# Accumulating DMAs for the row additions of a transformer layer, a fourth raw tile, and follow-ups beside two blocks

## The chip, the core and the metric

The kernel runs on one core of a Trainium2 chip. The engines of the core work side by side, each through its own instruction queue in order: PE multiplies matrices, DVE (vector), ACT (scalar) and POOL (GpSimd) work on rows, SP issues DMAs. An instruction that waits for a semaphore holds up everything behind it on its queue. The metric is the device time of one execution in microseconds, lower is better.

## The reference

One layer in float32 over 2048 tokens of width 1024: a token mixer (sliding-window attention and a gated recurrence side by side), a cross-attention into 256 memory tokens, and a SwiGLU feed-forward part of width 2816. Each part sits between two RMS norms and is added to the residual stream `h`:

```python
y = jnp.concatenate([ya, yh.astype(ya.dtype)], axis=-1) @ w_out[l]
h = h + rms_norm(y, g_mix_post[l])
u = rms_norm(h, g_x_pre[l])
m = rms_norm(mem, g_mem[l])
y = cross_attention(u, m, wq_x[l], wk_x[l], wv_x[l], wo_x[l])
h = h + rms_norm(y, g_x_post[l])
u = rms_norm(h, g_ffn_pre[l])
y = (jax.nn.silu(u @ w_gate[l]) * (u @ w_up[l])) @ w_down[l]
h = h + rms_norm(y, g_ffn_post[l])
```

The three residual additions, and the sum over three chunks of the last product, are what the change moves to other hardware.

## The kernel before

**Arithmetic.** Every float32 operand of a matmul is split into a high and a low half of a reduced format (`split2`: the high half on ACT or POOL at L833 and L835, the low half, a subtraction, always on DVE at L836), and a product is three matmuls (L913 to L915). Operands called T (weights or feed-forward inputs) are built ahead and stay for a job; operands called S are streamed.

**Jobs and blocks.** From about 780 us on the program runs a list of jobs (`jobs`, `phases`): the mixer's output product, the attention scores, the attention values, the hidden layer for each half of the tokens (100% PE-bound, 1400 to 2200 us), and three down jobs, one for each chunk of the hidden width (6, 8 and 8 tiles of 128). Each of the first three and of the down jobs has eight blocks of 256 tokens. A block is a 2 x 2 scheme of matrix blocks: kind "s" uses seven products (Strassen-like, `seven`) with steps 1, 5, 6, 3, 7, 2, 4; kind "p" uses the plain eight in four steps (`eight`) and stands at the ends of jobs. `out(i, j, a, b)` empties one quarter of the result (two parts `a` and `b`) into row tiles `y[0]`, `y[1]` of 128 x 1024; the last quarter comes in the last step.

**Order around a block.** At the head of a block `stream` asks for the raw input of the next block: two tiles of 128 x 4 x 256 (`sraw`, three buffers). After each product step `upto` makes the S operands that are needed two steps on, one step of the follow-up generator of the block before (`after`) is taken, and half an operand T of a later step is built (`half`, out of row tiles that SP loads). A follow-up is drained at the end of the block beside which it ran. All row tiles come out of one pool of ten. This is program order; the framework's scheduler arranges each engine's queue after its own simulation, so that neighbours on a queue can stand the other way round.

**What the follow-ups do.** `mixed_block`: after the squares of the quarters ACT has the sums; POOL multiplies each quarter with the gain (`scaled`, L1187); then DVE scales by the inverse root and adds the residual row tile `x`, loaded by SP (L1210); the row goes to `h1_d`; ACT squares it again; PE transposes it (L1098) into the former `x` tile, and it goes to `h1t_d`. `value_block` is the same with `h1_d` as the residual (L1283), `h2_d` as the store, and a scaled copy in the former `x` tile (L1290) that is transposed to `u_d`. `down_block(c, ...)`: job 0 stores its rows to `y2_d`; job 1 loads those rows and adds them on POOL (L1388), then stores; job 2 loads and adds them on POOL, squares on ACT (L1161), loads the residual from `h2_d`, multiplies by gain and root on DVE (L1408), adds on POOL (L1409) and stores to the output, both in halves of 512 columns (`ffn_out`). The very last block (`end`) takes the rows of `y2_d` as an addend of the eviction on DVE (L930, L1364), and ends with a short chain: squares on ACT, two small operations and a power on POOL (L90, L92, L97), DVE, store.

All DMAs before are issued by SP (`load`, `store`).

Of the kernel before, what the change touches and what calls it, by code (L numbers as in the profile page):

```python
# [11 lines left out]
F32 = mybir.dt.float32  # L12
# [6 lines left out]
P = 128  # L19
T = 2048  # L20
D = 1024
# [27 lines left out]
class Layer:  # L49
# [137 lines left out]
    def mix(self):  # L187
        tc, I = self.tc, self.I
        kw = dict(reuse_waits="tile")
        with contextlib.ExitStack() as left:  # L190
# [5 lines left out]
            with (  # L196
# [5 lines left out]
                self.banks(at, "ps1", **MOST)  # L202
                u = self.in_first()
# [32 lines left out]
            with (  # L236
# [5 lines left out]
                self.banks(at, "ps3", **MOST)  # L242
                for _ in phases:
                    pass
# [621 lines left out]
    def streamed(self, load, nk, kind, engine=None):  # L866
# [3 lines left out]
        for j in range(2):  # L870
            self._n += 1
            t = self.ts.tile([P, 4, 256], F32, tag="raw", name=f"sraw_{self._n}", bufs=3)[:, :nk, :]
            load(t, j)
            raw.append(t)
# [105 lines left out]
    def phases(self, jobs, first, prologue=None):  # L980
# [105 lines left out]
        for _ in after:  # L1086
            pass
# [91 lines left out]
    def scaled(self, d, a, b, to, g):  # L1179
# [7 lines left out]
        nc.gpsimd.tensor_tensor(d, d, g, ALU.mult)  # L1187

    def mixed_block(self, n):
        nc = self.nc  # L1190
        y, x, ss = {}, {}, []

        def out(i, j, a, b):
# [9 lines left out]
            sl = slice(j * 512, (j + 1) * 512)  # L1203
            self.scaled(y[i][:, sl], a, b, ss[0][:, 2 * i + j:2 * i + j + 1], self.g_mix_post[:, sl])

        def after():
            r = self.rstds(ss[0])
            s2 = self.small("q_s", 4)
            for i in range(2):
                nc.vector.scalar_tensor_tensor(y[i], y[i], r[:, i:i + 1], x[i], ALU.mult, ALU.add)  # L1210
                self.store(self.h1_d[(n + i) * P:(n + i + 1) * P, :], y[i])
                yield
            for i in range(2):
# [4 lines left out]
            for i in range(2):  # L1218
                self.store_transposed(self.h1t_d, n + i, self.transposed(y[i], x[i]))
# [40 lines left out]
    def value_block(self, n):  # L1260
        nc = self.nc
        y, x, ss = {}, {}, []

        def out(i, j, a, b):
# [8 lines left out]
            if (i, j) == (0, 0):  # L1273
                for r in range(2):
                    x[r] = self.rows_of(self.h1_d, n + r)
            sl = slice(j * 512, (j + 1) * 512)
            self.scaled(y[i][:, sl], a, b, ss[0][:, 2 * i + j:2 * i + j + 1], self.g_x_post[:, sl])

        def after():
            r = self.rstds(ss[0])  # L1280
            s2 = self.small("q_s", 4)
            for i in range(2):
                nc.vector.scalar_tensor_tensor(y[i], y[i], r[:, i:i + 1], x[i], ALU.mult, ALU.add)  # L1283
# [148 lines left out]
```

## Time and profile before

| | us |
|---|---|
| median of three runs | 2697.66 (2691.52 to 2702.04) |
| the profiled execution | 2689.73 |
| its span | 2688.0 |
| mean granted clock of PE | 0.989 |
| DMA queue of SP: 450 MB | 51.2% of 16 engines' span |

Times in the profile's rows are microseconds from the start of the span. A row of the timeline gives start, duration, engine, line, operation, output and inputs, the count of merged instructions, and in brackets how long the engine had been idle and what ended that. A group row gives busy us and mean ns of one instruction, then the idle time before it and its releasers. A row `A <- B: t, n, m` of the waits says that A waited for B for t us in all, n times, at most m. A window row gives start and end, its length, and the busy time of each engine with its number of instructions. An issue row of the DMAs gives KB each and median us from issue to landing. `Lnnn` is a line of the kernel; DMAs issued by the helpers carry the helpers' lines L75 (load) and L78 (store).

### The profile page before, as it was taken

The page shows a single profiled execution, that of the slowest core. Times are in us where ns is not written, and L with a number is a line of the kernel's source. Part 1 is how long each engine was busy: PE and PEld are TensorE (multiplying, and loading weights), DVE is VectorE, ACT ScalarE, POOL GpSimd, SP SyncE. Part 2 cuts the span into 40 slices and gives each one's busy share as a digit, 9 for nine tenths or more (in the row PEclk, how much of TensorE's full clock was granted, in tenths as well). Part 3 has the DMA queues.
Part 4 walks back from the last instruction along what each step waited for, and adds up shares of the span by engine and source line. Part 5 has one row for each costly group of instructions (what it writes and reads, how often), then busy time and mean ns, then how long its engine had stood idle before and what let it go on. Part 6 is the DMA issues. An engine that isn't in the chain of part 4 may idle for free. (4 is left out here: it accounts for less than half of the span.)

```text
span 2688.0 us, 34731 instructions
## 1 busy us (share of the span) xinstructions
PE 2590.8 (96%) x12362; PEld 2155.6 (80%) x12362; DVE 1804.5 (67%) x2653; ACT 1236.4 (46%) x2585; POOL 660.7 (25%) x733
## 2 busy tenths in 40 slices
PE   7989999999989999999999999999999999999987
PEld 5878888887977787887778888888888888888765
DVE  7675578877545668687785555575555565676987
ACT  4453366655424566555563333353333343533432
POOL 5340344322533552234420000000000000032455
PEclk9999999999999999999999999999999999999998
DMA  5434655445878585385772222362222253846654
GB/s 176 137 124 165 191 155 159 131 142 170 252 238 243 194 288 190 111 265 190 247 252 79 86 90 81 96 235 86 79 79 87 87 197 131 290 168 249 237 185 167
DMA packets 396429, 452.26 MB, mean 168 GB/s; under 512 B 19296, under 2 KB 310112, under 8 KB 396256
## 3 DMA queue, kind: packets, MB, share of 16 engines
q1 hardware_dynamic: 396256, 450.05, 51.2%
q8 instruction: 97, 1.59, 0.3%
q14 instruction: 76, 0.62, 0.1%
HBM read 315.77 MB, written 134.22 MB: 167 GB/s over the span
## 5 line engine op out<-in xcount | busy, mean ns | idle before, releaser
L913 PE MATMUL psm<-T,S 128*128 128x512 f32 x2726 | 1064.4, 394 | 27.0 <-ACT part L928 13.4
L915 PE MATMUL psm<-T,S 128*128 128x512 f32 x2726 | 1058.8, 392 | 16.7 <-DVE S L836 16.6
L914 PE MATMUL psm<-T,S 128*128 128x512 f32 x2726 | 1066.5, 391 | 0.8 <-DVE T L836 0.8
L913 PEld LDWEIGHTS psm<-T,S 128*128 128x128 f32 x2726 | 514.9, 189 | 142.3 <-ACT part L928 17.2
L915 PEld LDWEIGHTS psm<-T,S 128*128 128x128 f32 x2726 | 515.2, 189 | 130.7 <-DVE S L836 23.2
L914 PEld LDWEIGHTS psm<-T,S 128*128 128x128 f32 x2726 | 515.2, 189 | 106.7 <-DVE T L836 1.4
L836 DVE TENSOR_TENSOR S<-sraw,S 128x512 fp32r<-128x512 f32 (+1 forms) x327 | 277.5, 856 | 230.9 <-ACT S L833 214.6
L1388 POOL TENSOR_TENSOR row<-row,row 128x1024 f32<-128x1024 f32 x30 | 84.6, 2829 | 1140.6 <-DVE row L856 980.6
L833 ACT ACTIVATE S<-sum 128x512 fp32r<-128x512 f32 (+1 forms) x288 | 173.0, 617 | 344.2 <-PE psm L915 247.2
L836 DVE TENSOR_TENSOR S<-sum,S 128x512 fp32r<-128x512 f32 (+1 forms) x340 | 249.3, 741 | 48.9 <-ACT S L833 30.4
L928 ACT ACTIVATE part<-psm 128x512 f32<-128x512 f32 x252 | 149.7, 596 | 214.5 <-PE psm L915 197.2
L833 ACT ACTIVATE S<-sraw 128x512 fp32r<-128x512 f32 (+1 forms) x274 | 168.6, 615 | 131.0 <-PE psm L915 119.4
L836 DVE TENSOR_TENSOR T<-row,T 128x1024 fp32r<-128x1024 f32 (+1 forms) x134 | 166.5, 1251 | 55.7 <-ACT T L833 54.7
L833 ACT ACTIVATE T<-row 128x1024 fp32r<-128x1024 f32 (+1 forms) x134 | 136.7, 1030 | 117.4 <-DVE row L853 25.8
L151 PE MATMUL psg<-u,whi 128*128 128x512 f32 x352 | 142.1, 404 | 1.7 <-POOL whi L135 1.7
L153 PE MATMUL psg<-u,wlo 128*128 128x512 f32 x352 | 140.2, 398 | 0.9 <-DVE wlo L136 0.9
L152 PE MATMUL psg<-u,whi 128*128 128x512 f32 x352 | 140.0, 398 | 0.0
L1161 ACT ACTIVATE junk<-row 128x512 f32<-128x512 f32 x160 | 99.8, 625 | 74.5 <-POOL row L1388 27.3
L1187 POOL TENSOR_TENSOR row<-row,g 128x512 f32<-128x512 f32 x64 | 97.8, 1537 | 111.2 <-ACT junk L1161 103.2
L888 DVE TENSOR_TENSOR sum<-sraw,sraw 128x512 f32<-128x512 f32 (+1 forms) x85 | 61.3, 721 | 43.3 <-DMA sraw<-hid_d 9.0
L1311 DVE TENSOR_TENSOR row<-psm,part 128x512 f32<-128x512 f32 x60 | 39.9, 688 | 68.3 <-PE psm L915 68.3
L135 POOL TENSOR_SCALAR whi<-raw 128x1024 fp32r<-128x1024 f32 x46 | 52.4, 1139 | 126.8 <-PE psg L152 36.4
(328 smaller groups left out, 3688.8 us busy)
## 6 DMA issues: line engine op xcount, KB each, us to landing
row<-in_w_down_dram SPq DMA_DIRECT2D x53, 512.0 KB, 7.0
sraw<-in_w_gate_dram SPq DMA_DIRECT2D x44, 512.0 KB, 3.8
row<-u_d SPq DMA_DIRECT2D x44, 512.0 KB, 7.6
sraw<-in_w_up_dram SPq DMA_DIRECT2D x44, 512.0 KB, 3.7
hid_d<-row SPq DMA_DIRECT2D x44, 512.0 KB, 2.6
h_d<-row SPq DMA_DIRECT2D x32, 512.0 KB, 2.7
row<-h_d SPq DMA_DIRECT2D x32, 512.0 KB, 5.9
y_d<-row SPq DMA_DIRECT2D x32, 512.0 KB, 3.5
```

Of the source, the lines that this page charges most:

```text
L151: nc.tensor.matmul(ps, ah, bh, start=(i == 0), stop=False)
L152: nc.tensor.matmul(ps, ah, bl, start=False, stop=False)
L153: nc.tensor.matmul(ps, al, bh, start=False, stop=(i == n - 1))
L833: self.nc.scalar.activation(hi, raw, AF.Copy)
L836: self.nc.vector.tensor_tensor(lo, raw, f32(hi), ALU.subtract)
L913: nc.tensor.matmul(ps, s[:, 0, k, :], t[:, 0, k, :], start=st, stop=False, **kw)
L914: nc.tensor.matmul(ps, s[:, 0, k, :], t[:, 1, k, :], start=False, stop=False, **kw)
L915: nc.tensor.matmul(ps, s[:, 1, k, :], t[:, 0, k, :], start=False, stop=sp, **kw)
L928: nc.scalar.activation(t, ps, AF.Copy)
L1161: self.nc.scalar.activation(junk, a, AF.Square, scale=float(D) ** -0.5, accum_out=to)
L1187: nc.gpsimd.tensor_tensor(d, d, g, ALU.mult)
L1388: nc.gpsimd.tensor_tensor(y[i], y[i], y2[i], ALU.add)
```

## The change

- A new helper `add` issues, from POOL's queue, a DMA that reads rows from HBM and adds them to a row tile already in SBUF. It takes the place of the loads of residual rows and of `y2_d` rows, and of the POOL additions at L1388 and L1409. Before it stands the DVE pass that applies root and gain in one instruction, and after it the store, which waits for it.
- The POOL gain multiply in `scaled` (L1187) goes; the function is called `squared` and the gain is applied in the DVE pass.
- Raw tiles: four buffers in the second part of the program instead of three; row tiles: nine instead of ten (both are 4 KB in a partition).
- Follow-ups form a list: each step takes one step of every follow-up still alive, and a follow-up isn't drained at the end of a block. The generators get empty steps between the additions and the squares, and in `value_block` before the transposes.
- In the last down job the last two blocks (`late`) take the `y2_d` rows as addends of the eviction instead of an accumulating DMA; the residual of the last block is still loaded and added on DVE. The last chain on POOL has two operations instead of three.

```diff
@@ mix
                 self.banks(at, "ps3", **MOST)
+                self.raws = 4
@@ phases
-        after = iter(())
+        after = []
...
                     for _ in range(1 if kind == "s" else 2):
-                        next(after, None)
+                        for f in list(after):
+                            if next(f, after) is after:
+                                after.remove(f)
                         half(g, self.row_tile)
                     g += 1
-                for _ in after:
-                    pass
-                after = follow()
+                after.append(follow())
@@ row_tile
-        return self.st_pool.tile([P, D], F32, tag="row", name=f"row_{self._n}", bufs=10)
+        return self.st_pool.tile([P, D], F32, tag="row", name=f"row_{self._n}", bufs=9)
@@ squared
         self.mean_square(d, to)
-        nc.gpsimd.tensor_tensor(d, d, g, ALU.mult)
+
+    def add(self, d, src, n):
+
+        self.nc.gpsimd.dma_start(d, src[n * P:(n + 1) * P, :], accum_op=ALU.add)
@@ mixed_block
-            if (i, j) == (0, 0):
-                for r in range(2):
-                    x[r] = self.rows_of(self.I["x"], n + r)
...
             for i in range(2):
-                nc.vector.scalar_tensor_tensor(y[i], y[i], r[:, i:i + 1], x[i], ALU.mult, ALU.add)
+                nc.vector.scalar_tensor_tensor(y[i], y[i], r[:, i:i + 1], self.g_mix_post, ALU.mult, ALU.mult)
+                self.add(y[i], self.I["x"], n + i)
                 self.store(self.h1_d[(n + i) * P:(n + i + 1) * P, :], y[i])
                 yield
+            yield
             for i in range(2):
                 self.mean_squares(y[i], i, s2)
                 yield
...
-                self.store_transposed(self.h1t_d, n + i, self.transposed(y[i], x[i]))
+                self.store_transposed(self.h1t_d, n + i, self.transposed(y[i], self.row_tile()))
@@ value_block
-                nc.vector.scalar_tensor_tensor(y[i], y[i], r[:, i:i + 1], x[i], ALU.mult, ALU.add)
+                nc.vector.scalar_tensor_tensor(y[i], y[i], r[:, i:i + 1], self.g_x_post, ALU.mult, ALU.mult)
+                self.add(y[i], self.h1_d, n + i)
                 self.store(self.h2_d[(n + i) * P:(n + i + 1) * P, :], y[i])
-                self.mean_squares(y[i], i, s2)
-                yield
-            r = self.rstds(s2)
+                yield
             yield
             for i in range(2):
-                nc.vector.scalar_tensor_tensor(x[i], y[i], r[:, i:i + 1], self.g_ffn_pre, ALU.mult, ALU.mult)
-                yield
+                self.mean_squares(y[i], i, s2)
+                yield
+            r = self.rstds(s2)
+            u = [self.row_tile() for _ in range(2)]
             for i in range(2):
-                self.store_transposed(self.u_d, n + i, self.transposed(x[i], x[i]))
+                nc.vector.scalar_tensor_tensor(u[i], y[i], r[:, i:i + 1], self.g_ffn_pre, ALU.mult, ALU.mult)
+                yield
+            yield
+            for i in range(2):
+                self.store_transposed(self.u_d, n + i, self.transposed(u[i], u[i]))
                 yield
@@ down_block
+        late = last and n >= NT - 4
...
-            if end:
+            if late:
                 for i in range(2):
                     y[i] = self.rows_of(self.y2_d, n + i)
...
-            elif end:
+            elif late:
                 nc.vector.tensor_tensor(d, a, d, ALU.add)
...
-                    r = self.rstd([ss[0][:, 2 * i + q:2 * i + q + 1] for q in range(2)], 1, "p")
+                    v = self.small("p_v")
+                    nc.gpsimd.tensor_scalar(v, ss[0][:, 2 * i:2 * i + 1], ss[0][:, 2 * i + 1:2 * i + 2], EPS,
+                                            ALU.add, ALU.add)
+                    r = self.small("p_r")
+                    nc.gpsimd.tensor_tensor(r, v, self.mhalf[:, 0:1], ALU.pow)
...
-                if y2:
-                    nc.gpsimd.tensor_tensor(y[i], y[i], y2[i], ALU.add)
...
+            for i in range(0 if late else 2):
+                if c:
+                    self.add(y[i], self.y2_d, n + i)
+                if not last:
+                    self.store(self.y2_d[(n + i) * P:(n + i + 1) * P, :], y[i])
+                yield
+            if last:
+                if not late:
+                    yield
+                for i in range(2):
                     self.mean_squares(y[i], i, s2)
...
+                yield
                 r = self.rstds(s2)
                 for i in range(2):
-                    self.ffn_out(n + i, y[i], x[i], r[:, i:i + 1])
+                    nc.vector.scalar_tensor_tensor(y[i], y[i], r[:, i:i + 1], self.g_post, ALU.mult, ALU.mult)
+                    self.add(y[i], self.h2_d, n + i)
+                    self.store(self.out[(n + i) * P:(n + i + 1) * P, :], y[i])
                     yield
 
-        return stream, out, after, part if end else None
+        return stream, out, after, part if late else None
```

More of the change, by code (lines that the diff above doesn't have):

```diff
@@ L871, in streamed @@
             self._n += 1
-            t = self.ts.tile([P, 4, 256], F32, tag="raw", name=f"sraw_{self._n}", bufs=3)[:, :nk, :]
+            t = self.ts.tile([P, 4, 256], F32, tag="raw", name=f"sraw_{self._n}", bufs=self.raws)[:, :nk, :]
             load(t, j)
@@ L1078, in phases @@
                     for _ in range(1 if kind == "s" else 2):
-                        next(after, None)
+                        for f in list(after):
+                            if next(f, after) is after:
+                                after.remove(f)
                         half(g, self.row_tile)
                     g += 1
-                for _ in after:
-                    pass
-                after = follow()
+                after.append(follow())
                 at += 1
-        for _ in after:
-            pass
+        for f in after:
+            for _ in f:
+                pass
     def transposed(self, y, t):
@@ L1272, in out @@
                     self.load(self.g_ffn_pre, self.I["g_ffn_pre"][0:1, :].broadcast_to([P, D]))
[L1273 to L1277, printed above, removed]
+            self.squared(y[i][:, j * 512:(j + 1) * 512], a, b, ss[0][:, 2 * i + j:2 * i + j + 1])
         def after():
@@ L1353, in out @@
                 y[i] = self.row_tile()
-            if c and not end and (i, j) == (0, 0):
-                for r in range(2):
-                    y2[r] = self.rows_of(self.y2_d, n + r)
             if end and not x:
```

26 lines of the change are left out of this document (7 added, 19 removed).

## The prediction

> **What bounds it.** I read the page's 40 slices first, then windows of 20 us, then the rows inside the bad windows.
>
> ```profile
> span 2688.0 us, 34731 instructions
> PE   7989999999989999999999999999999999999987
> POOL 5340344322533552234420000000000000032455
> ```
>
> PE is full nearly everywhere, so only stretches where it waits can be won. POOL returns in the last slices, where PE dips. The windows there (length, then busy us and instructions of PE, PE's weight loads, DVE, ACT and POOL; granted clock, DMA share, GB/s):
>
> ```profile
> 2500.00:2520.00 20.00, 20.00 (x90) 16.57 (x89) 17.71 (x17) 10.27 (x15) 7.76 (x2) 1.00 0.80 290
> 2520.00:2540.00 20.00, 15.37 (x59) 11.28 (x58) 19.88 (x21) 9.60 (x20) 12.67 (x9) 0.91 0.37 130
> 2540.00:2560.00 20.00, 20.00 (x90) 16.55 (x89) 17.83 (x18) 9.17 (x19) 12.41 (x9) 1.00 0.41 147
> 2560.00:2580.00 20.00, 17.58 (x77) 13.96 (x75) 15.82 (x14) 8.24 (x18) 11.44 (x9) 1.00 0.55 198
> 2580.00:2600.00 20.00, 16.54 (x71) 12.97 (x71) 15.92 (x17) 8.09 (x18) 10.08 (x8) 1.00 0.50 184
> 2600.00:2620.00 20.00, 16.49 (x70) 12.66 (x69) 16.81 (x16) 7.73 (x17) 11.06 (x8) 1.00 0.52 188
> 2620.00:2640.00 20.00, 16.40 (x69) 12.60 (x68) 16.05 (x16) 6.04 (x13) 11.79 (x8) 0.97 0.63 233
> 2640.00:2660.00 20.00, 20.00 (x78) 16.24 (x77) 15.19 (x16) 6.87 (x16) 12.20 (x9) 0.86 0.52 189
> 2660.00:2680.00 20.00, 14.23 (x54) 11.15 (x52) 14.61 (x15) 5.29 (x16) 11.38 (x11) 0.83 0.27 104
> ```
>
> The first is a full window: 90 matmuls in 20 us, 0.222 us each. The eight after it, the last down job, hold 59+90+77+71+70+69+78+54 = 568, worth 126.2 us at that pace; they take 160. So this job loses 33.8 us. Part of it shows as a lowered clock behind a gap, not as idle time, so I count matmuls.
>
> One such gap, then the engine groups from 2120 us on (busy us, mean ns):
>
> ```profile
> 2588.97 5.56 POOL L1388 TENSOR_TENSOR row<-row,row 128x1024 f32<-128x1024 f32 x2 [7.29 <-DMA row<-y_d]
> 2589.43 6.24 DVE L836 TENSOR_TENSOR S<-sraw,S 128x512 fp32r<-128x512 f32 x3
> 2592.32 0.50 PE L915 MATMUL psm<-T,S 128*128 128x512 f32 x1 [2.63 <-DVE S L836]
> 2666.66 4.78 DVE L1408 SCALAR_TENSOR_TENSOR row<-row,q_r,g 128x512 f32<-128x512 f32 x4 [0.69 <-POOL q_r L1176]
> 2667.49 6.30 POOL L1409 TENSOR_TENSOR row<-row,row 128x512 f32<-128x512 f32 x4 [0.87 <-DVE row L1408]
> 2675.09 0.77 PE L913 MATMUL psm<-T,S 128*128 128x512 f32 x1 [5.77 <-DVE row L1362]
> ...
> L836 DVE TENSOR_TENSOR S<-sraw,S 128x512 fp32r<-128x512 f32 x66 | 79.2, 1218 | 28.3 <-ACT S L833 28.1
> L888 DVE TENSOR_TENSOR sum<-sraw 128x512 f32<-128x512 f32 x16 | 11.0, 685 | 0.2
> L1408 DVE SCALAR_TENSOR_TENSOR row<-row,q_r,g 128x512 f32<-128x512 f32 x28 | 33.6, 1261 | 6.0 <-POOL q_r L1176 6.0
> L1409 POOL TENSOR_TENSOR row<-row,row 128x512 f32<-128x512 f32 x28 | 47.2, 1716 | 6.7 <-DVE row L1408 6.7
> ```
>
> While POOL adds two rows, three DVE subtractions take 6.24 us; alone one takes about 0.685, so 2.06. DVE stands still beside a POOL add, the low half of S comes late, and PE waits 2.63 us. The 5.77 us gap has the same neighbour: four gain multiplies on DVE beside four additions on POOL (L1408, L1409), and behind them on DVE the eviction that PE waits for.
>
> SP adds to it. Its waits between 2540 and 2680 us, and two blocks' first loads:
>
> ```profile
> SPq L78 <- POOL row L1409: 61.9, 20, 13.4
> ...
> 2582.89 0.38 SPq L75 DMA_DIRECT2D sraw<-hid_d  x1
> 2606.32 0.38 SPq L75 DMA_DIRECT2D sraw<-hid_d  x1
> ```
>
> Output stores block the queue until L1409 is done and the next raw tile is asked for behind them. A block takes 23.43 us; its 84 matmuls (7 products of 4 x 3) need 18.7.
>
> **The change, part by part.** *POOL row additions out* (L1388, L1409; L1187 in the two earlier jobs). In the last job a block drops about 2 x 2.8 + 4 x 1.7 = 12.4 us of POOL work. What ended PE's waits there was a DVE result late beside POOL, so most of the 33.8 us is within reach. I leave 3 us of the first window (new weights are built there, DVE 19.88 of 20 busy), 1 us in each of five blocks and 2 us at the end: 33.8 - 10 = **24 us won**. Bounds: 33.8 if all goes, 0 if DVE is held as long by what replaces it. Next in line is PE itself: undisturbed, DVE has 14 operations of 0.69 and two of 1.28 us in a block, 12.2 of 18.7.
>
> In the value job a block is 21.82 us:
>
> ```profile
> 1237.66 0.37 SPq L75 DMA_DIRECT2D sraw<-pt_d  x1
> 1259.48 0.37 SPq L75 DMA_DIRECT2D sraw<-pt_d  x1
> ...
> 1379.29 1.03 PE L1098 MATMUL pss<-ident,row 128*128 128x128 f32 x8
> L1283 DVE SCALAR_TENSOR_TENSOR row<-row,q_r,row x16: 1272/1280/1637, 1209.2 to 1366.7; 128x1024 f32<-128x1024 f32 x16
> L1187 POOL TENSOR_TENSOR row<-row,g 128x512 f32<-128x512 f32 x64 | 97.8, 1537 | 111.2 <-ACT junk L1161 103.2
> ```
>
> 84 matmuls and 16 transposes need 18.7 + 2.1 = 20.8 us, so 1.0 us is lost in each of six steady blocks. The four gain multiplies go off POOL and ride free in the DVE pass that added the residual (1.28 us, as L1283 now). I take half: **3 us** (0 to 6). The mixed job runs at full pace after 880 us; its one stall follows here, and I take 0 for it (0 to 5.5), since ACT stood there behind a weight tile that SP asked for only at 870.10:
>
> ```profile
> PE psm L913 <- ACT part L928: 5.5, 1, 5.5
> 870.10 0.37 SPq L75 DMA_DIRECT2D row<-in_w_out_dram  x1
> ```
>
> *74 accumulating DMAs in* (16 mixed, 16 value, 16 in the second down job, 12 + 14 in the last), issued from POOL. They replace as many 512 KB loads on SP, so HBM traffic stays. The trace has no such DMA. From below it is a plain load, from above two of the slowest, as it must read both sums: h_d rows land in 5.9 us, u_d rows in 7.6.
>
> ```profile
> row<-u_d SPq DMA_DIRECT2D x44, 512.0 KB, 7.6
> row<-h_d SPq DMA_DIRECT2D x32, 512.0 KB, 5.9
> out_dram<-row SPq DMA_DIRECT2D x32, 256.0 KB, 2.0
> ```
>
> So 5.9 to 15.2 us; I take 9, a load and a half, because these loads already share the engines. On POOL the issue costs at most what a small operation does (L90 0.76 us, below); it waits there for the DVE pass, and behind it on POOL stand the splits of S (L835) that the mixed and value jobs give to POOL. L1187 waited there for ACT instead, so I put the difference at 0.
>
> *New waits.* Two queues now wait for a landing. On ACT the squares (L1161): behind them stand the high halves of S and the copies that free PSUM. The code leaves three product steps between add and square in mixed and value, two for the second row in the last job, and S is made two steps ahead. A step is 12 x 0.222 = 2.67 us, so PE feels a landing later than 5 x 2.67 = 13.3 us, or 4 x 2.67 = 10.7. At 9 us nothing shows; I charge **2 us** for uneven landings (0 to 57, the top worked out below). On SP the stores wait for the landing; behind them stand raw and weight loads. The fourth raw tile lets both loads of a block go out a block ahead, 18.7 us against a 9 us hold: 0, but without that cover the late loads cost what they cost now, some of the 4.7 us a block.
>
> *The rest.* Nine row tiles for ten: a block no longer holds two residual tiles, so no tile is missed; 0. Follow-ups beside two blocks: only value's is longer than a block; its transposes move three steps on, and the next job reads the early blocks first; 0. The late blocks' addend goes to DVE's eviction as the last block's did; 0 with POOL quiet. The final chain drops one POOL operation:
>
> ```profile
> 2681.81 0.76 POOL L90 TENSOR_SCALAR p_v<-q_s 128x1 f32<-128x1 f32 x1 [3.67 <-ACT junk L1161]
> 2682.65 0.22 POOL L92 TENSOR_SCALAR p_w<-p_v 128x1 f32<-128x1 f32 x1
> ```
>
> 0.3 us. **Sum:** 24 + 3 - 2 + 0.3 = 25 us, span 2688 to 2663. That execution took 2689.73 us; the median of the runs, 2697.66, lies 7.9 above it. Taking the same 25 off the median gives 2672.
>
> The Trainium skill says, in SBUF — State Buffer, Who interferes with whom, that a DVE instruction with two SBUF inputs contends with a GpSimd instruction that reads SBUF; the 6.24 us above agree. The same page, SBUF: two separate sides, speaks against the change: descriptors of a GpSimd DMA are written by GpSimd and starve while DVE runs a 2-port operation, for which it gives about 3.1 us instead of 0.62. By that every add could come some 2.5 us later, an estimate from that page; 9 + 2.5 = 11.5 would touch only the last job.
>
> **Rivals.** *More than forecast:* the value loss and the mixed stall go whole, and the last job runs nearly clean: 33.8 + 6 + 5.5 = 45, so 2652. For: late weight rows came from a crowded row pool. Against: those jobs keep ACT and DMA as busy.
>
> *Given back:* stores that wait for landings hold SP so long that raw tiles stay late, and each of five or six blocks keeps its 4.7 us; the early jobs lose a little too. Net about -3, 2695. For: SP's 61.9 us behind L1409. Against: the fourth tile.
>
> *Slower:* the add is as slow as its upper bound, 15.2 us. ACT then stalls 15.2 - 13.3 = 1.9 us in 16 blocks and 4.5 us in six: 57 us against the 27 won, so +30 and 2728. It decides from 13.8 us of landing, where 16 x (L - 13.3) + 6 x (L - 10.7) is 27. For: in the mixed job the engines are already 78% busy:
>
> ```profile
> 880.00:1020.00 140.00, 140.00 (x667) 116.20 (x667) 93.78 (x102) 82.60 (x184) 71.33 (x91) 1.00 0.78 261
> ```
>
> Against: the last job's share is near 0.5.
>
> *It doesn't do what it says:* issuing a DMA holds DVE as an add did. At 0.76 us for four issues instead of 12.4 us that can keep at most a quarter; if issues were as long as L1409's 1.7, half the gain: 2686.
>
> **Numbers.** Forecast 0.60, more 0.10, given back 0.12, slower 0.14, no relief 0.04. What a measurement can tell from no change is 0.5%, 13.5 us. Faster: nearly all of 0.60, 0.10 and part of the last: 0.70. Same: 0.15, slower: 0.15. The likeliest case alone spans 2660 to 2686; the range reaches to the clean case below (2649) and partly into the slow one above, 2706.
>
> **What would show it.** Right: L836 and the gain multiplies near 0.69 and 1.3 us throughout, 84-matmul blocks of 19 to 20 us in the last job, no PE wait on L836 there, adds landing under 11 us. Wrong: PE or ACT waiting on rows that an add writes, SP stores held over 10 us, DVE operations still double.

## The result, and the profile after

The changed kernel takes 2686.02 us (median of 9 runs, 2680.87 to 2690.87) against 2698.03 (9 runs): a ratio of 0.9955, 95% interval 0.9942 to 0.9969. Forecast were 25 us (2672), measured are 12. The page of the changed kernel (span; POOL in 40 slices; packets, MB and share of each DMA queue, q1 for SP and q0 for POOL):

```profile
span 2683.9 us, 34591 instructions
...
POOL 5240344321431332223320000000000000000022
...
q1 hardware_dynamic: 383584, 411.25, 47.4%
q0 software_dynamic: 10656, 38.80, 8.2%
```

POOL is quiet in the last job now. Its windows, in the columns of the prediction:

```profile
2520.00:2540.00 20.00, 18.27 (x81) 14.81 (x79) 13.22 (x14) 9.41 (x13) 1.19 (x2) 1.00 1.03 339
2540.00:2560.00 20.00, 16.35 (x63) 13.37 (x64) 14.78 (x20) 10.17 (x20) 2.82 (x6) 0.83 0.51 112
2560.00:2580.00 20.00, 20.00 (x90) 16.56 (x89) 12.41 (x18) 9.84 (x21) 5.71 (x9) 1.00 0.88 213
2580.00:2600.00 20.00, 20.00 (x90) 16.55 (x89) 12.54 (x18) 9.05 (x19) 4.96 (x8) 1.00 0.88 214
2600.00:2620.00 20.00, 20.00 (x90) 16.57 (x89) 12.73 (x19) 9.05 (x19) 5.10 (x8) 1.00 1.03 272
2620.00:2640.00 20.00, 20.00 (x90) 16.58 (x89) 10.67 (x15) 8.45 (x18) 4.75 (x7) 1.00 0.96 253
2640.00:2660.00 20.00, 20.00 (x90) 16.57 (x89) 14.39 (x22) 9.04 (x21) 3.80 (x6) 1.00 0.84 197
2660.00:2680.00 20.00, 14.05 (x61) 11.00 (x60) 12.94 (x19) 4.95 (x14) 5.67 (x9) 0.94 0.80 216
```

From 2560 to 2660 us every window holds the full 90 matmuls, where before had 69 to 78. The engine groups from 2120 us on say why: the subtraction that took 1218 ns in the mean with POOL's additions beside it (L836, now L838) takes 690, and a pass over twice the columns with gain and root takes 1280, where the half pass took 1261.

```profile
L838 DVE TENSOR_TENSOR S<-sraw,S 128x512 fp32r<-128x512 f32 x69 | 47.1, 690 | 55.9 <-ACT S L835 55.8
L1407 DVE SCALAR_TENSOR_TENSOR row<-row,q_r,g 128x1024 f32<-128x1024 f32 x14 | 17.8, 1280 | 4.4 <-POOL q_r L1179 4.1
L1193 POOL DMA_DIRECT2D row<-h_d x14 | 12.8, 917 | 12.7 <-DVE row L1407 12.1 <-DVE S L838 0.6
```

The last row is the issue of an add: 0.92 us of POOL. The landings of the adds (KB each, median us):

```profile
row<-h_d POOLq DMA_DIRECT2D x30, 512.0 KB, 7.7
row<-y_d POOLq DMA_DIRECT2D x28, 512.0 KB, 6.8
row<-in_x_dram POOLq DMA_DIRECT2D x16, 512.0 KB, 7.7
```

The slowest of them took 12.2 us. In the last job nearly all this is as forecast or better, so something ahead of it was lost. It shows at the two places where a job hands over to the next: mixed to score, and value to hidden. Windows over the two, for the kernel before (a second execution, see below) and then for the changed one:

```profile
968.00:1068.00 100.00, 97.80 (x460) 79.95 (x459) 78.53 (x105) 60.28 (x129) 37.26 (x51) 1.00 0.75 255
1323.00:1433.00 110.00, 105.82 (x481) 85.47 (x480) 87.89 (x94) 63.97 (x119) 27.17 (x30) 1.00 0.70 238
```

```profile
968.00:1068.00 100.00, 91.61 (x421) 74.74 (x420) 67.77 (x83) 58.43 (x120) 32.40 (x45) 0.95 0.91 273
1323.00:1433.00 110.00, 100.12 (x449) 81.04 (x448) 75.29 (x84) 61.67 (x118) 20.82 (x32) 0.95 0.83 257
```

39 and 32 matmuls fewer in the same time, 71 x 0.222 = some 15.8 us, with the clock down behind the gaps and the share of the DMA engines up from 0.75 to 0.91 and from 0.70 to 0.83. What stood behind the gaps in the changed kernel's timeline:

```profile
1044.25 0.80 PE L915 MATMUL psm<-T,S 128*128 128x512 f32 x1 [4.99 <-ACT T L835]
...
1380.80 1.94 PE L1101 MATMUL pss<-ident,row 128*128 128x128 f32 x8 [3.68 <-ACT T L835]
1396.83 1.23 DVE L852 TENSOR_TENSOR row<-row,row 128x1024 f32<-128x1024 f32 x1 [4.04 <-DMA row<-u_d]
1405.58 0.79 PE L915 MATMUL psm<-T,S 128*128 128x512 f32 x1 [3.55 <-ACT S L835]
```

At the first hand-over PE waits for an operand T of the next job. T is built out of row tiles that SP loads (for the score job of `qk_d`, for the hidden job of `u_d`), and these land late. At the second the view names T in front of a transpose and S in front of a matmul; T and the high half of S are made on ACT's queue, which stands there for rows of `u_d` (7.9 us in all from 1340 to 1430).

**Where the time went, by stretch.** Cutting every profile into windows of 4 us and adding up their matmuls gives the time at which each kernel had done the same number of them (a matmul on a border counts twice, in all alike). The table gives, for each stretch (times are those of the reference execution), what a kernel lost (+) or won (-) against a second profiled execution of the kernel before (span 2690.7); the column of the last job is what is left to the difference of the spans. The experiments follow below.

| | to 779 | mixed to 968 | hand-over to 1144 | value to 1323 | hand-over to 1509 | to 2502 | last job | ratio of the runs |
|---|---|---|---|---|---|---|---|---|
| before, first execution | -5.7 | +0.1 | -1.2 | -0.3 | +1.2 | -1.0 | +4.2 | |
| changed | +6.8 | -0.6 | +8.5 | -5.4 | +9.2 | -2.3 | -23.0 | 0.9955 |
| e1 down jobs only | +5.7 | +0.8 | +0.4 | +0.6 | +2.6 | -0.9 | -22.2 | 0.9936 |
| e2 front jobs only | +3.4 | -2.0 | +7.6 | -4.6 | +8.1 | -0.4 | -4.7 | 1.0011 |
| e3 ten rows, three raws | +6.5 | -0.1 | +7.4 | +5.3 | +3.5 | -0.7 | -23.1 | 0.9986 |
| e4 before, nine rows, four raws | +2.5 | +1.1 | +2.9 | +2.3 | +0.6 | +0.1 | -1.1 | 1.0010 |
| e5 late stores in front | -2.3 | -2.0 | +7.5 | -4.9 | +9.7 | -0.9 | -22.4 | 0.9956 |
| e6 plain loads in front | +2.5 | -1.1 | +1.3 | -4.9 | +0.5 | -0.7 | -20.5 | 0.9888 |
| e8 down jobs only, late stores | +0.2 | +2.7 | +1.3 | +0.8 | +1.3 | +0.9 | -26.3 | 0.9942 |
| e9 plain loads and copies | +1.4 | -2.0 | +2.9 | +6.5 | +8.8 | -0.8 | -21.9 | 0.9985 |
| e10 early adds | +6.8 | +2.1 | +3.8 | -4.7 | +6.9 | -0.7 | -26.0 | 0.9925 |
| e11 early adds in value only | +8.6 | +1.5 | +1.6 | -4.8 | +6.5 | -0.9 | -28.6 | 0.9934 |
| e12 order only | +4.7 | +2.9 | +4.1 | +4.4 | +2.7 | -3.7 | -22.3 | 0.9943 |
| e13 early adds, order of before | +6.7 | -1.4 | +1.8 | -5.7 | +6.9 | -0.7 | -22.1 | 0.9911 |
| e14 stores from ACT | +8.7 | -2.6 | +11.4 | +4.6 | +10.0 | -3.0 | -20.3 | 0.9995 |
| e15 e13, stores from ACT | +0.6 | -0.2 | +2.8 | +1.6 | +6.8 | -0.7 | -21.1 | 0.9945 |

In the first 779 us, where the edits hardly touch the program, executions lie 14 us apart, so I read from there on: the changed kernel wins 23.0 + 5.4 + 0.6 + 2.3 = 31.3 and loses 17.7 at the hand-overs, together 13.6. The medians say 12.0. Each row is one execution. How far a figure scatters is seen in the two executions of before (1.2 us at a hand-over, 4.2 in the last job) and in e5, whose stores turned out to stand where those of the changed kernel do (0.5 to 1.0 at the hand-overs). The cut at 779 us falls where PE waits, so the first two columns of a row can trade some 2 us.

The second hand-over has to be read together with the value job before it. The changed kernel wins 5.4 there and loses 9.2 behind it, 3.8 in all; e1, with no lead from the value job, loses 3.2 in all, and e6 wins 4.4. So against before, more than half of the 9.2 takes back what the value job had won; against plain loads in the same places the adds cost 3.8 + 4.4 = 8.2 us there, and 8.5 - 1.3 = 7.2 at the first hand-over.

### The profile page after: what moved, and what is told of

It is laid out like the page before. It is cut to its first block, busy times and chain, and to the rows that moved or that the text cites. A ratio compares the mean times of both kernels' runs of the same rounds, so it can differ in the third digit from the quotient of the medians.

```text
span 2683.9 us, 34591 instructions
## 1 busy us (share of the span) xinstructions
PE 2588.4 (96%) x12362; PEld 2162.3 (81%) x12362; DVE 1691.2 (63%) x2643; ACT 1236.3 (46%) x2581; POOL 500.3 (19%) x683
## 4 chain that ended last, share of the span: by engine, by line
PE 79%; DMA 9%; DVE 3%; POOL 3%; issue 3%; ACT 2%; SPq 1%; POOLq 0%; DVEq 0%; ACTq 0%
PE psm L917 21%; PE psm L915 21%; PE psm L916 21%; PE psg L153 2%; PE psg L151 2%; PE psg L152 2%; DMA row<-in_w_down_dram 1%; PE pss L1101 1%; DMA row<-h_d 1%; DMA row<-in_w_out_dram 1%; DMA row<-in_x_dram 1%; DMA z<-in_w_out_dram 1%; DMA row<-u_d 1%; DVE S L838 0%; DMA h1t_d<-row 0%
## 5 line engine op out<-in xcount | busy, mean ns | idle before, releaser
L838 DVE TENSOR_TENSOR S<-sraw,S 128x512 fp32r<-128x512 f32 (+1 forms) x327 | 228.8, 704 | 253.8 <-ACT S L835 234.4
L838 DVE TENSOR_TENSOR S<-sum,S 128x512 fp32r<-128x512 f32 (+1 forms) x340 | 229.6, 685 | 62.7 <-ACT S L835 38.9
L930 ACT ACTIVATE part<-psm 128x512 f32<-128x512 f32 x249 | 147.5, 597 | 224.5 <-PE psm L917 209.3
L1193 POOL DMA_DIRECT2D row<-y_d x28 | 25.9, 926 | 1136.8 <-DVE T L838 971.7
L838 DVE TENSOR_TENSOR T<-row,T 128x1024 fp32r<-128x1024 f32 (+1 forms) x134 | 159.0, 1193 | 75.4 <-ACT T L835 74.3
L136 DVE TENSOR_TENSOR wlo<-raw,whi 128x1024 fp32r<-128x1024 f32 x46 | 59.6, 1295 | 38.3 <-POOL whi L135 36.5
L915 PE MATMUL psm<-u,S 128*128 128x512 f32 x172 | 68.8, 403 | 11.5 <-POOL u L837 8.5
L1325 DVE TENSOR_TENSOR part<-psm,part 128x512 f32<-128x512 f32 x60 | 39.7, 688 | 63.4 <-PE psm L917 63.4
```

The lines of the kernel that those rows point to most:

```text
L136: (lo_engine or nc.vector).tensor_tensor(lo, raw, f32(hi), ALU.subtract)
L838: self.nc.vector.tensor_tensor(lo, raw, f32(hi), ALU.subtract)
L915: nc.tensor.matmul(ps, s[:, 0, k, :], t[:, 0, k, :], start=st, stop=False, **kw)
L930: nc.scalar.activation(t, ps, AF.Copy)
```

## The experiments

**e1 to e4: which part costs.**

```diff
 # e1: mixed_block and value_block as before, ten row tiles, three raw tiles
 # e2: down_block as before
 # e3: changed kernel
-        self.raws = 4        ... bufs=9
+        self.raws = 3        ... bufs=10
 # e4: the kernel before
-  row bufs=10, sraw bufs=3
+  row bufs=9,  sraw bufs=4 (second part)
```

> Accumulating DMAs in the down jobs alone: the mixed and value jobs are those of before (POOL multiplies the gain, SP loads the residual), with ten row tiles and three raw tiles as before; the list of follow-ups and the late blocks stay. Theory (the last job won what was forecast, and the jobs ahead of it gave most of it back): the jobs up to 2500 us take what they took before, the last job wins 24 to 28 us, about 25 us faster than before (2673), 13 faster than the changed kernel. Rival (the fourth raw tile is what covers the stores that wait in the last job): without it half of the gain there goes, 10 to 15 us faster than before, no better than the changed kernel.

> The other half: accumulating DMAs in the mixed and value jobs alone, nine row tiles and four raw tiles, the down jobs as before. Theory: this half costs, 10 to 20 us slower than before, lost where one job hands over to the next and ahead of 800 us. Rival (what the two profiles show before 1420 us is the scatter between executions): within 4 us of before.

> The changed kernel with the 4 KB of a partition given back: ten row tiles, three raw tiles. Theory A (weights come late at the hand-overs because row tiles are short): the hand-overs from mixed to score and from value to the hidden job win 8 to 15 us, the changed kernel minus 8 to 15 in all, less what the last job loses without the fourth raw tile. Theory B (SP stands behind stores that wait for an add): the hand-overs stay as slow as in the changed kernel. Theory C (the fourth raw tile's early loads push back the weights ahead of 800 us): the 8 us between 700 and 780 us come back, whatever the hand-overs do.

> The kernel before with nothing but nine row tiles and four raw tiles. Theory A (row tiles are short): the hand-overs lose 10 us or more, 10 to 20 slower than before. Theory B (stores that wait for adds): the hand-overs are those of before. Theory C (early raw loads ahead of 800 us): 5 to 10 slower, all of it ahead of 800 us.

Measured: e1 2679.86 us, ratio 0.9936 (0.9921 to 0.9952), no slower than the whole change, with three raw tiles; that is 17 us of the 25 expected. e2 2698.95, 1.0011 (1.0000 to 1.0021), not the 10 to 20 us slower that were expected: the front jobs' adds bring nothing, since what the value job wins goes at the hand-overs. e3 2692.15, 0.9986 (0.9975 to 0.9997): ten row tiles don't mend the first hand-over, and with three raw tiles the value job loses 5.3 us instead of winning 5.4. So the fourth raw tile earns its place there (with nine row tiles against ten), and not in the last job. e4 2698.7, 1.0010 (1.0001 to 1.0019): nine row tiles and four raw tiles alone cost a little, 2.9 us at the first hand-over and not the 10 of theory A.

**e5 to e8: held queue or busy engines.** Two theories were left. B: SP stands at a store that waits for its add, with weight loads behind it. C: an add holds the DMA engines much longer than a plain load, and at a hand-over, where the engines are full, the rows for the next operands land later. C has a row: q0 carries the adds alone, 74 of 144 packets each, so one takes 8.2% x 16 x 2683.9 / 74 = 47.6 engine-us. (An engine-us is the time that packets took on one of the 16 engines. Since windows have shares of up to 1.05, packets can overlap, so it is a price to compare with others and not a time in which an engine does nothing else.)

```diff
 # e5 (mixed, value); e8 the same in e1's down jobs
                 self.add(y[i], ...)
-                self.store(self.h1_d[...], y[i])
...
                 self.mean_squares(y[i], i, s2)
+                self.store(self.h1_d[...], y[i])
 # e6 (mixed, value)
-                self.add(y[i], ...)       # dma_start(d, src, accum_op=ALU.add)
+                self.plain(y[i], ...)     # dma_start(d, src)
 # e7: the kernel before, unchanged
```

> The changed kernel, but in the mixed and value jobs the store of an added row is issued two to three steps of its list later, beside the row's squares, so that SP reaches it after the add has landed. Against the kernel before's execution the changed kernel loses 7 us where the mixed job hands over to the score job (at equal count of matmuls, 1020 to 1080 us) and 7 to 8 us where the value job hands over to the hidden job (1316 to 1442 us). Theory B (SP stands at a store that waits for its add, and the loads of the next job's weights stand behind it on SP): both losses fall to the 1 to 1.5 us of the kernel with adds in the down jobs alone, and the time is 2686 - 12 = about 2674. Theory C (the adds themselves hold the DMA engines about 1.8 times as long as a plain load of the same 512 KB, and the weights land late for that): both losses stay at 7, time 2686 within 3. Theory A (nine row tiles too few): later stores hold row tiles longer, the losses grow, 2690.

> The changed kernel with the adds of the mixed and value jobs replaced by plain loads of the same rows on the same queue into the same tiles (these two sums are left out: the row of x or h1 takes the place of the sum); everything waits as before. Theory C (engine time of the read-modify-write): a transfer falls from some 48 engine-us to some 26, the losses at the two hand-overs fall from 7 and 8 to 1 to 3 us, time about 2675. Theory B (SP behind a store that waits for the transfer): the landing is perhaps 2 us sooner of 7, so the losses stay at 5 to 7 each, time 2683 to 2686.

> The kernel before, profiled a second time, as a yardstick for the first 780 us, where its program and the changed one hardly differ and every other kernel's execution stands 5 to 12 us behind the first profile of before. If that profile was a quick execution, this one stands 4 to 10 us behind it at the matmul count of 773 us and has a span of 2692 to 2702; if the first 780 us are really changed by the edit, it stands within 2 us of it.

> Adds in the down jobs alone (2680 measured), with the stores of the sums issued two steps later, when the adds have landed, so SP is not held before them. If SP's stands at these stores (about 10 us a block) make the last job's weights late (a 5.4 us wait of TensorE at its start in the changed kernel), 2674 to 2677; if the lead of the loads covers them, 2680 within 2; if the ten row tiles then run short because they are held longer, 2683 to 2688.

e5 took 2681.6 us, 0.9956 (0.9940 to 0.9972), e8 2678.7, 0.9942 (0.9920 to 0.9964): as their parents. But of SP's hold they tell nothing. The scheduler had put the stores back at their old places on SP's queue, and SP's waits show it, in the changed kernel and in e5 (in the last job it is 104.1 us in e1 and 101.9 in e8):

```profile
SPq L78 <- DMA row<-in_x_dram: 65.4, 14, 14.6
```

```profile
SPq L78 <- DMA row<-in_x_dram: 65.8, 14, 14.0
```

An edit of program order is no edit of a queue until the queue has been looked at.

e6 took 2663.2 us, 0.9888 (0.9862 to 0.9913): (0.9955 - 0.9888) x 2697 = 18 us off the changed kernel, and both hand-overs are clean (+1.3 and +0.5 us). It leaves out two sums, so its time is a probe and no version to use. Its page and its windows:

```profile
q0 software_dynamic: 10656, 38.80, 6.3%
```

```profile
968.00:1068.00 100.00, 97.56 (x458) 80.58 (x457) 74.44 (x96) 64.11 (x136) 32.39 (x48) 0.98 0.83 278
1323.00:1433.00 110.00, 106.54 (x480) 87.40 (x479) 77.59 (x90) 62.12 (x117) 14.96 (x24) 0.97 0.73 248
```

The price of a plain load follows from three pages. e1's q0 has its 42 adds of the down jobs alone:

```profile
q0 software_dynamic: 6048, 22.02, 4.5%
```

4.5% x 16 x 2677.7 / 42 = 45.9 engine-us. e6's q0 has these 42 and 32 plain loads: (6.3% x 16 x 2667.8 - 42 x 45.9) / 32 = 23.8. So an add is two plain loads, and 16 of them in a front job are 16 x (47.6 - 23.8) / 16 = 24 us more of all 16 engines, ahead of and beside the loads for the next job. Windows in which the engines are full show a lower rate with adds (last two columns: share, GB/s), the changed kernel and then e6:

```profile
1020.00:1040.00 20.00, 19.26 (x89) 15.68 (x88) 11.96 (x14) 6.25 (x15) 3.26 (x6) 1.00 1.05 315
...
1380.00:1400.00 20.00, 19.20 (x86) 16.24 (x87) 11.56 (x12) 7.69 (x14) 4.65 (x5) 0.91 1.05 316
```

```profile
1000.00:1020.00 20.00, 20.00 (x98) 16.73 (x97) 14.06 (x15) 12.01 (x26) 8.71 (x13) 1.00 1.04 382
...
1360.00:1380.00 20.00, 20.00 (x98) 16.73 (x97) 14.05 (x14) 10.46 (x22) 5.45 (x8) 1.00 1.05 373
```

Over all windows of 20 us from 960 to 1400 us with a share of 0.98 or more it is 269 to 345 GB/s in the changed kernel and e5, and 328 to 387 in e6, e1 and the two executions of before, which have no add there. So the adds go with a lower rate, but a full share has no one rate: full windows ahead of 860 us carry 244 to 307 without any add. And the plain loads also land sooner, so SP's hold shrank with them (65.4 to 46.3 us for the rows of x), and B is not excluded by e6.

e7, the yardstick, took 2692.42 us with a span of 2690.7, just under the 2692 to 2702 expected; at 779 us it stands 5.7 us behind the first profile of before, as expected of a quick first execution.

**e9 to e11: the engine time put back, and the adds moved off the hand-overs.**

```diff
 # e9: e6, and behind each plain load
+        if n >= 2:
+            self.nc.gpsimd.dma_start(to[n * P:(n + 1) * P, :], src[(n - 2) * P:(n - 1) * P, :])
 # e10 (mixed, value); e11: value only, mixed_block as before
+        late = n >= NT - 6
...
+                if late:
+                    nc.vector.scalar_tensor_tensor(y[i], y[i], r[:, i:i + 1], x[i], ALU.mult, ALU.add)
+                else:
                     nc.vector.scalar_tensor_tensor(y[i], y[i], r[:, i:i + 1], g, ALU.mult, ALU.mult)
                     self.add(y[i], ...)
```

> The kernel with plain loads in place of the adds in the front jobs (2663 measured, both hand-overs without loss), and behind each load a second transfer of 512 KB on the same queue that nothing waits for: a copy of the row stored one block before into a place in DRAM that is never read. Nothing in the kernel's waits changes; the DMA engines alone get more work, by about what an add takes over a plain load (48 against some 26 engine-us). Theory C (engine time at a stretch where the DMA is full): the losses of 7 to 9 us at each of the two hand-overs come back, time 2676 to 2684. If it was the latency of the read-modify-write, or its order against the plain transfers, and not its engine time: at most 2 us each, 2663 to 2668.

> The changed kernel, but the last three of the eight blocks of the mixed and of the value job load their rows and sum on DVE and scale on POOL, as before; the first five keep the accumulating adds. Theory C: the stretches of full DMA at the two hand-overs are rid of most adds, the losses there fall from about 9 us each to 1 to 3, and the value job keeps more than half of its 5 us: 2686 - 12 = 2672 to 2676. If the loss comes from something else in the changed functions (nine row tiles, follow-ups run later), it stays: 2683 to 2687.

> As the kernel with early adds, but the mixed job is that of before altogether, since it won nothing there. By theory C: no loss at the first hand-over, 1 to 3 us at the second, 3 to 5 won in the value job, 17 to 20 in the last down job: about 2674, within 3 us of the kernel with early adds and some 5 us below the kernel with adds in the down jobs alone. If nine row tiles hurt the mixed job of before: a loss of 3 to 4 us at its hand-over, 2678.

e9 took 2691.74 us, 0.9985 (0.9973 to 0.9998): (0.9985 - 0.9888) x 2697 = 26 us of e6's gain gone by copies whose result nothing waits for. That is 8 us beyond what theory C had expected. Its q0:

```profile
q0 software_dynamic: 11552, 53.48, 7.9%
```

(7.9% x 16 x 2685.6 - 6.3% x 16 x 2667.8) / 28 = 25 engine-us a copy, so load and copy weigh what an add does. The second hand-over loses 8.8 us again, the first only 2.9, and the value job loses 6.5 where it won 4.9. But the run is not engine time alone: the copies themselves wait on POOL's queue, for stores to `h1_d` or `h2_d` (both printed as `h_d`), in the mixed stretch (780 to 1144 us) and then the value stretch (1144 to 1520):

```profile
POOL sx_d L1204 <- DMA h_d<-row: 51.0, 12, 7.9
```

```profile
POOL sh_d L1204 <- DMA h_d<-row: 43.2, 10, 7.4
```

Behind them on POOL stand high halves of S and the next row loads, so the value job's loss can be POOL's hold. At the second hand-over PE's longest waits are for operands T out of rows of `u_d` (1340 to 1430 us):

```profile
PE psm L917 <- ACT T L837: 7.3, 2, 3.7
```

That fits transfers that land late and engines that are busy, but POOL's hold ahead of it is not excluded. At the first hand-over the copies gave back 2.9 - 1.3 = 1.6 us of 7.2, so engine time of this size is not shown to make that loss.

e10 took 2678.98 us, 0.9925 (0.9909 to 0.9941), e11 2679.3, 0.9934 (0.9921 to 0.9948): e10 better than the whole change, e11 by its median, with intervals that overlap; both some 3 to 5 us slower than expected. With no add in the last three blocks the first hand-over loses 3.8 and 1.6 us, but the second still 6.9 and 6.5: half a hit.

**e12 and e13: the order of the follow-ups.**

```diff
 # e12: e10 with no add in front jobs
-        late = n >= NT - 6
+        late = True
 # e13: e10, and for the late blocks no empty steps, value's squares beside the sum
-            yield
+            if not late:
+                yield
```

> The changed kernel with no add at all in the mixed and value jobs (all eight blocks load their rows and sum as before), but with the changed kernel's order of follow-up steps, its list of follow-ups, nine row tiles and four raw tiles in the value job; the down jobs keep their adds. It asks what is left of the 4 and 7 us that the kernel with early adds still loses at the two hand-overs. If that is the order of the follow-up steps (extra empty steps, h1T and u stored later): 4 and 6 to 7 us again, and nothing won in the value job, 2684 to 2688. If the early adds do it (they put the DMA's work back): 1 to 2 us at each, nothing won in the value job, about 2680, as with adds in the down jobs alone.

> The kernel with early adds, and its last three blocks of the mixed and value jobs also in before's order of follow-up steps (no empty steps, squares beside the sum, in the value job). If the order of the steps makes the losses left at the hand-overs: they fall from 4 and 7 us to 1 to 2 each, time 2669 to 2673, faster than every other version with the right sum. If the early adds make them, or the lead won in the value job is simply lost again because the next weights land when they land: unchanged, 2677 to 2681.

e12 took 2685.21 us, 0.9943 (0.9927 to 0.9960): without an add in front, the changed order with nine row tiles loses 4.1 us at the first hand-over and 4.4 in the value job. e13 took 2675.54, 0.9911 (0.9898 to 0.9924), the quickest with nothing left out, though its interval overlaps e10's: 1.8 us at the first hand-over against e10's 3.8. So there the order may take a share; the 2 us are not far from the 1.2 by which two executions of before differ. It is no fixed price, since e6 has the order of the changed kernel and loses 1.3. The second hand-over keeps its 6.9 us.

**e14 and e15: SP's hold taken away.**

```diff
 # e14: changed kernel; e15: e13, for the blocks with adds
                 self.mean_squares(y[i], i, s2)
-                self.store(self.h1_d[...], y[i])        # issued by SP
+                self.nc.scalar.dma_start(self.h1_d[...], y[i])   # by ACT
```

> The changed kernel with the stores of the added rows of the mixed and value jobs issued from ACT's queue, beside the squares that wait for the same add there, and not from SP. (In the kernel with late stores the scheduler had put these stores back at their old places on SP, and SP waited for the adds of x 65.8 us as before, so that run told nothing of SP.) The adds and the bytes stay. Theory B (SP held by stores that wait for the add's landing, weight loads behind them): SP's waits for added rows in these jobs go to 0, the losses at the two hand-overs fall from 8.5 and 9.2 us to 1 to 3, time 2670 to 2675. Theory C (engine time of the adds): they stay at 6 to 9, time 2684 to 2687. ACT held longer by the stores: above 2688.

> The kernel with early adds and before's order in the last three blocks (2675.5 measured), with the stores of its added rows issued from ACT. Theory B: what it still loses at the second hand-over (6.9 us) falls to about 2, 2670. Theory C: the adds stand far ahead of the hand-over and SP's stores there wait for DVE, so nothing changes, 2674 to 2678.

e14 took 2695.95 us, 0.9995 (0.9984 to 1.0007), e15 2683.07, 0.9945 (0.9933 to 0.9956). In e14 SP has no wait for an added row left in the front jobs, and the hand-overs still lose 11.4 and 10.0 us. But ACT now stands where SP stood. Its waits from 1144 to 1500 us, changed kernel and then e14:

```profile
ACT junk L1164 <- DMA row<-h_d: 7.3, 7, 1.8
```

```profile
ACT junk L1164 <- DMA row<-h_d: 25.8, 6, 9.2
```

From 780 to 1144 us e14's ACT waits for added rows in front of other work too, among it the halves of operands S; the changed kernel has no such wait:

```profile
ACT S L835 <- DMA row<-in_x_dram: 10.4, 2, 5.4
```

The scheduler set some stores ahead of the squares, the value job turns from -5.4 to +4.6, and in e15 from -5.7 to +1.6. So e14 does not decide between a held queue and busy engines: it took the hold from one queue and gave it to another. In e15, where the last three blocks have no add and SP holds no store for one, the second hand-over still loses 6.8 us where theory B had about 2; its time misses both theories. What the two runs do show is that ACT is no better place for these stores.

## What of the prediction held, and the step that failed

- **Last job, 24 us: right.** 23.0 measured, 20.3 to 28.6 in every version of the table with adds in the down jobs. The mechanism is the one given: DVE no longer stands beside POOL additions (690 ns against 1218). What is left of PE's waits there is one of 5.4 us at its start, for a copy out of PSUM (L930) on ACT's queue. It stands there behind an operand T that waited 2.1 us for DVE to combine its weight rows; that these had landed late (DMA share 1.03) is likely, not shown.
- **Value job, 3 us (0 to 6): right in size, for more than the reason given.** 5.4 won, but the gain multiplies off POOL are not enough for it: with three raw tiles and ten rows the job loses 5.3 (e3). Nor is the raw tile alone (e4, +2.3). And the next hand-over takes the lead back. The mixed job, 0: -0.6.
- **Landing, 9 us: right side.** 6.8 to 7.7, at most 12.2, so the slower rival, which began at 13.8, never came near. "At 9 us nothing shows" did not hold all the same: ACT's squares waited 15.3 us for added rows in the mixed stretch, and PE once for one. Both are signs that the prediction had named for being wrong. (The second stands where before had its stall of 5.5 us.)

```profile
ACT junk L1164 <- DMA row<-in_x_dram: 15.3, 7, 7.6
```

```profile
871.28 1.97 PE L1101 MATMUL pss<-ident,row 128*128 128x128 f32 x8 [4.74 <-DMA row<-in_x_dram]
```

- **Issue on POOL, at most 0.76 us: low.** 0.92, without effect: DVE's operations stayed at 690 ns, so the rival without relief falls too. The Trainium skill (SBUF — State Buffer, SBUF: two separate sides) warns that descriptors of GpSimd's DMAs starve while DVE runs a 2-port operation. No delay of the kind is seen here: e6's plain loads landed, from POOL, in 4.8 us for the rows of x, and SP's in the second execution of before in 6.2. But no run tells whether DVE ran such an operation beside an issue, so the warning isn't tested.

```profile
row<-in_x_dram POOLq DMA_DIRECT2D x16, 512.0 KB, 4.8
```

```profile
row<-in_x_dram SPq DMA_DIRECT2D x16, 512.0 KB, 6.2
```

- **The step that failed: "They replace as many 512 KB loads on SP, so HBM traffic stays", and with it "I charge 2 us for uneven landings".** The add was priced by when it lands and who waits for that; what it takes from other transfers was set to what the load took that it replaced. Its engine time is twice that (47.6 against 23.8 engine-us), and the two hand-overs, full of loads for the next job, lost 8.5 and 9.2 us where 2 had been charged for all new waits. The prediction even quoted DMA engines 78% busy in the mixed job, and used that only for the landing. That the adds make the loss is shown by plain loads in their places, which end it (e6) and win 18 us. By what they make it is in part argued: a plain load takes half the engine time, lands sooner and holds SP for less, all at once. Copies of equal engine time brought the second loss back, with POOL's queue held besides, and a fifth of the first (e9). So engine time is the likely cause at the second hand-over, and at the first no run separates it from the landing and the held queues.
- **"No tile is missed; 0", and follow-ups 0: low, in the first front stretch.** Nine row tiles and four raw tiles alone cost 2.9 us at the first hand-over (e4); with the new order and no add it is 4.1, and 4.4 in the value job (e12). In the changed kernel SP stood once, for 4.4 us between 1000 and 1046 us, with a load that waited for a store of rows to `h1t_d`. Ten row tiles (e3) still lose 7.4 there, so this is not the main part. These prices do not add up to the 8.5, and how much of it each cause holds in the presence of the other is not separated.
- **SP's stores, 0: right by result in the last job, open in front.** SP's stores stood up to 14.6 us behind adds in the mixed job and up to 11.1 in the last one (94.3 us in all there), over the 10 that the prediction had set as a sign of being wrong, and the last job won its 23 us all the same. The fourth raw tile is not what covers them there (e1 has three, holds SP for 104.1 us and wins 22.2).
- **Given back** was a rival at 2695 by SP's hold. Something was given back, and less, in the front jobs and not in the last one; whether SP's hold has a share there is not separated.

Open is the second hand-over of e10, e11, e13 and e15, 6.5 to 6.9 us with no add in the last three blocks. Where the value job has no lead, the loss is 2.6 to 3.5 in e1, e3 and e12. That fits a lead given back because the rows for the next job come when the DMA has brought them. But e6 kept both, with lighter transfers throughout, and e15 speaks against it: it has no lead (+1.6) and still loses 6.8. A rival that no run tests: in e10, e11, e13 and e15 the late blocks load their residual rows into two more row tiles, out of nine.

## What to carry to other kernels

Price a DMA twice: by its landing, for whoever waits on it, and by the engine time it takes, for the transfers behind it. A full share of the DMA engines is not by itself a loss: in the last job, from 2560 to 2660 us, it rose with the adds from between 0.50 and 0.63 to between 0.84 and 1.03, and no window lost a matmul. The loss showed where the engines were full and PE was about to need what was in flight, so look at the windows in which one stage's operands are fetched while another still runs. Accumulating DMAs paid here where they took additions from POOL that slowed the vector engine (the down jobs); at the hand-overs plain loads were cheaper. And when an experiment moves an instruction in the program, look at its queue before reading the time.

## What the runs showed of the hardware

An accumulating DMA of 512 KB from HBM into SBUF took 46 to 48 engine-us (e1, changed kernel), a plain one on the same queue 24 (e6), at a landing of 7.7 against 4.8 us (rows of x). With adds among its transfers the DMA moved 269 to 345 GB/s in full windows at the hand-overs, without them 328 to 387. With adds issued from POOL (0.92 us each) DVE's subtractions took 690 ns in the mean; with POOL's additions beside them 1218. And the first 779 us scatter: 5.7 us between two executions of before, 9 between the changed kernel and e5, whose programs are alike there, 14 over all profiles. That is of the size of the whole effect measured, so one pair of profiles could not have shown it.
